# Half 1 of the tokens projected first, MLP halves renamed, and the operands of the MLP's first turn split between its stages

## The chip, the cores and the metric

The kernel runs on one core of one Trainium2 chip. The metric is the device time of one execution in microseconds (us). The engines are TensorE (PE: matrix products and transposes; PEld is its weight load), VectorE (DVE), ScalarE (ACT), GpSimd (POOL) and SyncE (SP), which here issues nearly all DMAs. Each engine works through its own instructions in order and waits for semaphores of the others.

## The reference

One layer of a streaming encoder trunk on 1024 tokens of width 1024, in float32, with RMS norms ahead of each part:

```python
for _ in range(DEPTH):
    h = h + parallel_mixer(rms_norm(h, norm_mix_g), w_in, ...)
    h = h + memory_cross_attention(rms_norm(h, norm_xattn_g), rms_norm(mem, norm_mem_g), ...)
    u = jax.nn.relu(rms_norm(h, norm_mlp_g) @ mlp_w1)
    h = h + (u * u) @ mlp_w2
```

The mixer holds eight heads of forgetting attention and four of gated linear attention. The cross-attention has four heads of 256 and ends in `o @ wo`, a product of 1024 x 1024 x 1024. The MLP has a hidden width of 4096: `mlp_w1` is 1024 x 4096, `mlp_w2` 4096 x 1024, with a squared ReLU between.

## The kernel before

**Products.** Every float32 operand is split into a high and a low part (`evac_split`, `split_into`): ScalarE copies it into the high part (L1038), VectorE subtracts that to get the low part (L1039). A product is then three matmuls of 128 x 128 by 128 x 512: high by high (L107), high weight by low operand (L108), low weight by high operand (L109). Tokens stand on the free axis in two halves of 512, and `h[:, k, half]` is the block of 128 rows k of the residual.

**Order.** A tile framework schedules the program from the order in which it is written and its own model of durations. It fixes the order of instructions on each engine and puts in the waits. Tiles come from pools; a new tile in a pool, or in a room that a closed pool has left, waits until the readers of the old one are done. SyncE's DMAs wait in one queue in their order.

**Cross-attention** (`xattn`). Eight units (n, u), two heads by four quarters of the tokens, are attended in turn. Each writes its output to DRAM (`od`, L1003), split into `o` high and low. `load_o` reads one half of the tokens back as `oh`, `ol`.

**The o-projection** (`project_o_first`, `project_o_rest`). 16 blocks of 24 matmuls: weights `Wo` (rows 0 to 3 of h) and `W` (rows 4 to 7), each by two halves of the tokens. Before, half 0 is finished first, by both, and then half 1 by `W` (rows 4 to 7) and by `Wo` (rows 0 to 3). `finish` adds the squares of a block into `acc` (ScalarE L165, GpSimd L166), writes the block to DRAM for the last addition (`hd`), and scales it for the MLP (L883). `token_squares` reduces `acc` to a norm per token with four transposes (L173).

**The MLP** (`mlp`). Each product is a Winograd form of Strassen's scheme with seven products in place of eight (`products7`): the operand's quarters give b11, b21, b22 and t1 to t4, the weight's give a11, a12, a22 and s1 to s4, and `STAGES` lists which pairs are multiplied, in which order, and into which kind of bank (x, w or y; banks of a kind go on accumulating). A stage has two weights i and, in the first layer, 12 matmuls for each. The first layer has eight turns p of seven stages, 168 matmuls each. The second has five chunks of 4, 3, 3, 3 and 3 hidden blocks, each with two turns, 168 or 126 matmuls. `hidden` and `output` take each bank away after its stage; the first layer's output goes to DRAM (`ud`) and comes back as operands of the second. `weights7` loads a turn's two weight tensors into `raw7` (1 MB or 768 KB each), splits the quarters, and makes s1 to s4 with sums (L1065, L1066, L1071, L1072, on VectorE in the first layer, on GpSimd in the second). Its generator yields twice, and `prep` runs it whole.

**Operands of the first turn.** b11 and b21 are split as soon as half 0 is projected. Then come, in each of the last four blocks, L841 (the block's sum), L883, L909, L910, L913, L914 and L912 on VectorE, which make four of the operands in the room of h and the low part of t2. `mlp` then splits t1, t3, b22 and t4 whole (128 x 2048 each) before the first turn.

Of the kernel before, what the change touches and what calls it, by code (L numbers as in the profile page):

```python
# [51 lines left out]
class Layer:  # L52
# [798 lines left out]
    def project_o_rest(self, mx):

# [3 lines left out]
        with ExitStack() as st:  # L856
# [28 lines left out]
            for k in range(KT):  # L885
                finish(k, 0, h(k, 0), k == 0)
                if k % 4 == 3:
                    self.operand(("b11", "b21")[k // 4], x0, self.h[:, k - 3:k + 1, 0:512])
            self.token_squares(0, self.yv[:, 0:4])
# [10 lines left out]
            next(self.W1)  # L900

            X = self.X["t2"] = self.T(x0, [P, 2, 4, 512], F32R, "x7")
            for i in range(4):
# [1 line left out]
                self.o_block(self.Wo, 0, 1, i, next(banks), t)
                finish(i, 1, t, False)
                t2 = self.T(self.s7, [P, 2, 512], F32, "s7")[:, 0, :]
                b11, b21, b12, b22 = h(i, 0), h(4 + i, 0), h(i, 1), h(4 + i, 1)
                nc.vector.tensor_tensor(b11, b12, b11, ALU.subtract)  # L909
                nc.vector.tensor_tensor(t2, b22, b11, ALU.subtract)  # L910
                nc.scalar.activation(X[:, 0, i], t2, AF.Copy)
                nc.vector.tensor_tensor(X[:, 1, i], t2, f(X[:, 0, i]), ALU.subtract)  # L912
                nc.vector.tensor_tensor(b12, b22, b12, ALU.subtract)  # L913
                nc.vector.tensor_tensor(b21, b21, t2, ALU.subtract)  # L914
            self.XB["t2"] = [X[:, 0, i] for i in range(4)], [X[:, 1, i] for i in range(4)]
# [7 lines left out]
    def xattn(self):  # L923
        nc = self.nc
        with ExitStack() as st:
# [80 lines left out]
            units = [(n, u) for n in range(2) for u in range(4)]  # L1006
            q = []
            for i, (n, u) in enumerate(units):
                if u == 0:
# [32 lines left out]
    def weights7(self, srcs, n, eng):  # L1042
# [14 lines left out]
        for src, o in zip(srcs, out):  # L1057
            raw = self.T(self.raw7, [P, 4, 512], F32, "raw7")[:, :, 0:n]
            nc.sync.dma_start(raw, src)
# [206 lines left out]
```

## Time and profile before

| | |
|---|---|
| median of 3 runs | 1486.61 us (1486.08 to 1487.83) |
| the profiled execution | 1480.27 us |
| its span in the trace | 1478.6 us |
| mean granted TensorE clock | 0.988 |
| end of the o-projection, start of the MLP's first turn | about 847 us |
| DMA, mean over the span | 151 GB/s, 223.94 MB |

The trace is of one execution, and its times count from the start of the span. An engine's row gives the time in which it was busy; the granted clock is the share of full speed at which TensorE was allowed to run. A wait is put down to the instruction that released it, with the line of the kernel. Stretches of the span have their own busy times; a timeline lists single instructions with the idle time ahead of them in brackets.

### The profile page before, as it was taken

To read this page: it belongs to the slowest core of one execution; us is meant where nothing else is said; L and a number is where in the kernel's file an instruction comes from. 1 tells how busy PE (TensorE), PEld (TensorE's weight loads), DVE (VectorE), ACT (ScalarE), POOL (GpSimd) and SP (SyncE) were. 2 spreads that over 40 slices of the span, in tenths; PEclk is the share of its full clock that TensorE was granted. 3 is DMA by queue.
4 is the path that set the end of the run, shared out by engine and by line. 5 is a ranking of instruction groups with operands and counts; after the bars stand their busy time and mean duration, and the time that the engine had idled before them with its cause. 6 is when DMAs were issued, how large, how long until landed. Compare 5 with 4: busy or idle time off the path is not lost.

```text
span 1478.6 us, 19173 instructions
## 1 busy us (share of the span) xinstructions
PE 1430.0 (97%) x7058; PEld 1195.3 (81%) x7058; DVE 920.8 (62%) x1322; ACT 681.2 (46%) x1092; POOL 430.8 (29%) x457
## 2 busy tenths in 40 slices
PE   7999999999998998999999979999999999999998
PEld 6777788887887787888888868888888888888886
DVE  4396422427776676656654875765565848788686
ACT  4473332326776555445442344544444736335230
POOL 3157503323463412522212300000000342433454
PEclk9999999999999999999999989999999999999999
DMA  8424530259677752413285113544444846337353
GB/s 273 122 54 121 143 86 1 72 173 261 187 203 193 192 158 74 155 40 104 72 279 219 52 63 146 210 171 171 170 169 149 291 159 229 129 109 233 113 201 114
DMA packets 125118, 223.94 MB, mean 151 GB/s; under 512 B 8384, under 2 KB 66528, under 8 KB 118368
## 3 DMA queue, kind: packets, MB, share of 16 engines
q1 hardware_dynamic: 125024, 222.71, 47.0%
q8 instruction: 56, 0.92, 0.2%
q14 instruction: 38, 0.31, 0.1%
HBM read 150.59 MB, written 72.09 MB: 151 GB/s over the span
## 4 chain that ended last, share of the span: by engine, by line
PE 78%; DMA 8%; DVE 7%; ACT 3%; issue 1%; POOL 1%; SPq 0%; POOLq 0%; ACTq 0%; DVEq 0%
PE mm L107 13%; PE mm L108 12%; PE mm L109 12%; PE my L109 7%; PE my L107 7%; PE my L108 7%; PE tr L107 3%; PE tr L108 3%; PE tr L109 3%; DMA raw<-in_w_in_dram 2%; DMA raw<-in_xattn_wkv_dram 2%; PE tr L661 1%; PE pv L668 1%; PE pv L669 1%; PE s L621 1%
## 5 line engine op out<-in xcount | busy, mean ns | idle before, releaser
L109 PE MATMUL my<-x,g 128*128 128x512 f32 x472 | 184.7, 392 | 5.9 <-DVE g L1039 5.8
L107 PE MATMUL my<-x,g 128*128 128x512 f32 x472 | 185.0, 392 | 2.8 <-ACT g L1038 2.8
L108 PE MATMUL my<-x,g 128*128 128x512 f32 x472 | 184.6, 391 | 0.0
L1065 POOL TENSOR_TENSOR s<-raw 128x384 f32<-128x384 f32 (+1 forms) x20 | 25.9, 1297 | 372.0 <-DMA raw<-in_mlp_w_dram 341.4
L1038 ACT ACTIVATE g<-s 128x1024 fp32r<-128x1024 f32 (+1 forms) x72 | 69.0, 963 | 132.8 <-PE my L109 62.3
L108 PE MATMUL mm<-wl,xh 128*128 128x512 f32 x320 | 126.5, 396 | 3.6 <-DVE wl L97 3.6
L107 PE MATMUL mm<-wh,xh 128*128 128x512 f32 x320 | 127.4, 400 | 1.4 <-DVE sq L298 1.4
L109 PE MATMUL mm<-wh,xl 128*128 128x512 f32 x320 | 126.3, 395 | 0.0
L109 PEld LDWEIGHTS my<-x,g 128*128 128x128 f32 x472 | 89.1, 189 | 25.5 <-DVE g L1039 7.0
L107 PEld LDWEIGHTS my<-x,g 128*128 128x128 f32 x472 | 89.2, 189 | 21.8 <-ACT g L1038 3.0
L108 PEld LDWEIGHTS my<-x,g 128*128 128x128 f32 x472 | 89.2, 189 | 18.5
L1039 DVE TENSOR_TENSOR g<-s,g 128x1024 fp32r<-128x1024 f32 (+1 forms) x72 | 85.0, 1186 | 11.1 <-ACT g L1038 10.7
L107 PE MATMUL mm<-x,g 128*128 128x512 f32 x228 | 89.3, 392 | 0.0
L108 PE MATMUL mm<-x,g 128*128 128x512 f32 x228 | 89.2, 391 | 0.0
L109 PE MATMUL mm<-x,g 128*128 128x512 f32 x228 | 88.8, 390 | 0.0
L632 POOL TENSOR_SCALAR p<-p,rrec 128x128 f32<-128x128 f32 (+3 forms) x64 | 50.8, 796 | 128.0 <-DVE rrec L631 115.4
L1039 DVE TENSOR_TENSOR g<-raw,g 128x1024 fp32r<-128x1024 f32 (+3 forms) x72 | 65.4, 910 | 34.2 <-ACT g L1038 34.2
L1178 DVE TENSOR_TENSOR x<-x 128x1024 fp32r<-128x1024 f32 (+1 forms) x64 | 74.4, 1184 | 11.4 <-ACT x L1177 11.1
L97 DVE SCALAR_TENSOR_TENSOR wl<-raw,cols,wh 128x512 fp32r<-128x512 f32 x64 | 49.8, 816 | 48.0 <-ACT wh L96 42.8
L1038 ACT ACTIVATE g<-raw 128x1024 fp32r<-128x1024 f32 (+3 forms) x72 | 55.2, 769 | 48.2 <-PE my L109 20.6
L107 PE MATMUL mm<-wh,sh 128*128 128x512 f32 x192 | 76.3, 399 | 0.7 <-DVE mkv L118 0.4
L108 PE MATMUL tr<-x,g 128*128 128x512 f32 x196 | 76.2, 389 | 0.0
(309 smaller groups left out, 3786.5 us busy)
## 6 DMA issues: line engine op xcount, KB each, us to landing
ud<-h SPq DMA_DIRECT2D x32, 1024.0 KB
x<-ud SPq DMA_DIRECT2D x48, 512.0 KB
raw<-in_mlp_w_dram SPq DMA_DIRECT2D x20, 1024.0 KB
raw<-in_mlp_w_dram SPq DMA_DIRECT2D x16, 768.0 KB
raw<-in_w_in_dram SPq DMA_DIRECT2D x23, 512.0 KB
raw<-in_xattn_wkv_dram SPq DMA_DIRECT2D x16, 512.0 KB
od<-o SPq DMA_DIRECT2D x32, 256.0 KB
xt<-in_x_dram SPq DMA_DIRECT2D x8, 512.0 KB
```

Of the source, the lines that this page charges most:

```text
L97: nc.vector.scalar_tensor_tensor(wl, r, g, f(wh), ALU.mult, ALU.subtract)
L107: mm(ps, lh[k], rh[k], start=start and k == 0, stop=False, **kw)
L108: mm(ps, lh[k], rl[k], start=False, stop=False, **kw)
L109: mm(ps, ll[k], rh[k], start=False, stop=stop and k == n - 1, **kw)
L621: nc.tensor.matmul(ps[:, c], qa[:, ts], ka[:, c], start=True, stop=False)
L632: nc.gpsimd.tensor_scalar(p[:, 0:n], p[:, 0:n], rr, 1.0, ALU.mult, ALU.mult)
L661: nc.tensor.transpose(o, pp[i][:, kb * P:(kb + 1) * P], self.ident)
L668: nc.tensor.matmul(pv, va[:, kb, :], th[:, js], start=kb == 0, stop=False)
L1038: self.nc.scalar.activation(hi, src, AF.Copy)
L1039: self.nc.vector.tensor_tensor(lo, src, f(hi), ALU.subtract)
L1065: eng.tensor_tensor(s[:, 0], raw[:, 3], raw[:, 2], ALU.add)
L1178: nc.vector.tensor_tensor(lo, f(lo), f(hi), ALU.subtract)
```

## The change

Six things change together; every matrix product stays.

1. *Half 1 first.* The units of the second pair of heads are attended in the order 2, 3, 0, 1, `load_o` takes half 1 first, and the o-projection finishes half 1 before half 0. The last four blocks are rows 0 to 3 of half 0.
2. *Halves renamed.* The two halves of the MLP's inner dimension change names: b11 is now made of rows 4 to 7 of half 0 (before: rows 0 to 3), and the first layer's weights are stored in another order (`swapped`).
3. *b11 and t2 early.* Both are made and split block by block in the four blocks of `W` with half 0. The last four blocks only have their sum and their scaling.
4. *STAGES in another order*: before b11, b21, t2, t1, t3, b22, t4; now b11, t1, t2, b22, t3, b21, t4. `weights7` splits a11 first, then s1 and s2, s3 and s4, and a12 and a22 last; before, a11 and a12 came first and a22 last.
5. *Operands between the stages.* A generator `first_turn` splits t1 before the first turn and t3, b22, b21 and t4 after the first stages of it; `token_squares` of the last half moves to turn 1 and the spread of the factors F to turn 3.
6. *Rooms.* x0 has 2 tiles and x1 5 (before 3 and 4), `g74` opens earlier, and in the second layer the rooms are grouped as (b11, t1), (b22, t2), (b21, t3), (t4). The map from products to output quarters follows the new names.

```diff
-            self.load_o(op1, 1)
+            self.load_o(op1, 0)
             for i in range(4):
-                self.o_block(W, 1, 0, i, next(banks))
+                self.o_block(W, 1, 1, i, next(banks))
...
             for i in range(4):
                 t = self.T(xp, [P, 512], F32, "h2", bufs=2)
-                self.o_block(W, 1, 1, i, next(banks), t)
-                finish(4 + i, 1, t, i == 0)
+                self.o_block(W, 1, 0, i, next(banks), t)
+                finish(4 + i, 0, t, i == 0)
+                t2 = self.T(xp, [P, 512], F32, "t2", bufs=2)
+                b11, b12, b22 = h(4 + i, 0), h(4 + i, 1), h(i, 1)
+                self.evac_split(X1[:, 0, i], X1[:, 1, i], b11)
+                nc.vector.tensor_tensor(b11, b12, b11, ALU.subtract)
+                nc.vector.tensor_tensor(t2, b22, b11, ALU.subtract)
+                self.evac_split(X2[:, 0, i], X2[:, 1, i], t2)
+                nc.vector.tensor_tensor(b12, b22, b12, ALU.subtract)
...
-    STAGES = (("x", "a11", "b11"), ("w", "a12", "b21"), ("x", "s2", "t2"), ("y", "s1", "t1"), ("x", "s3", "t3"),
-              ("y", "s4", "b22"), ("x", "a22", "t4"))
+    STAGES = (("x", "a11", "b11"), ("y", "s1", "t1"), ("x", "s2", "t2"), ("y", "s4", "b22"), ("x", "s3", "t3"),
+              ("w", "a12", "b21"), ("x", "a22", "t4"))
...
-            g(o, ("a11", "a12"), raw[:, 0:2])
+            g(o, ("a11",), raw[:, 0:1])
             raws.append(raw)
-        yield
...
-            g(o, ("a22",), raw[:, 2:3])
-        yield out
+        for raw, o in zip(raws, out):
+            g(o, ("a12", "a22"), raw[:, 1:3])
+        yield
...
+        def first_turn():
+            self.operand("t1", x1, half(4, 0))
+            yield
+            self.operand("t3", x1, half(4, 1))
+            next(self.W1)
+            yield
+            self.operand("b22", x1, half(0, 1))
+            yield
+            t4 = half(0, 0)
+            self.operand("b21", x1, t4)
+            for j in range(2):
+                nc.vector.tensor_tensor(t4, t4, f(X["t2"][:, j]), ALU.subtract)
+            yield
+            self.operand("t4", x1, t4)
...
+            def taken(i, j, ps):
+                hidden(i, j, ps)
+                if p == 0 and i == 1:
+                    next(turn, None)
+
+            self.products7(A, B, 4, taken)
+            if p == 1:
+
+                self.token_squares(0, self.yv[:, 0:4])
```

In the fences below, x7 are operands, g1 and g2 weights split (one quarter, or a pair), s7 the weights' sums, raw7 the weights as loaded, and my and mm the banks of TensorE. Lines of the changed program are one or two lower than before for the same operation.

**TensorE, behind the first stages of the first turn.** Before, after b21 and the four transposes (x7_1876 is t2, x7_1903 is t1, g2_1894 and g2_1896 are s1 and s2 of the two weights):

```order
L109 MATMUL my_1910_8621<-x7_1858_8206,g2_1875_8360 128x512
L173 MATMUL tr_1913_8783<-ident_14_73,acc_1849_8161 128x128 [waits PE_49,Pool_49]
L173 MATMUL tr_1913_8783<-ident_14_73,acc_1849_8161 128x128 x3
L107 MATMUL my_1907_8579<-x7_1876_8363,g2_1894_8540 128x512 [waits Activation_49]
L108 MATMUL my_1907_8579<-x7_1876_8363,g2_1894_8540 128x512
L107 MATMUL mm_1911_8661<-x7_1903_8567,g2_1894_8540 128x512
L108 MATMUL mm_1911_8661<-x7_1903_8567,g2_1894_8540 128x512 [waits DVE_49]
L107 MATMUL my_1908_8593<-x7_1876_8363,g2_1896_8546 128x512 [waits Activation_49]
L108 MATMUL my_1908_8593<-x7_1876_8363,g2_1896_8546 128x512
L107 MATMUL mm_1912_8675<-x7_1903_8567,g2_1896_8546 128x512
L108 MATMUL mm_1912_8675<-x7_1903_8567,g2_1896_8546 128x512
L109 MATMUL my_1907_8579<-x7_1876_8363,g2_1894_8540 128x512 [waits DVE_49]
```

The changed program, from the last matmul of b11 on (x7_1896 is t1, g2_1881 and g2_1883 are s1 and s2 of the two weights):

```order
L109 MATMUL my_1898_8565<-x7_1859_8211,g1_1879_8391 128x512
L107 MATMUL my_1906_8600<-x7_1896_8548,g2_1881_8397 128x512 [waits DVE_49,Activation_49]
L107 MATMUL my_1907_8614<-x7_1896_8548,g2_1883_8403 128x512 [waits DVE_49]
L108 MATMUL my_1906_8600<-x7_1896_8548,g2_1881_8397 128x512 [waits DVE_49]
L109 MATMUL my_1906_8600<-x7_1896_8548,g2_1881_8397 128x512
L107 MATMUL my_1906_8600<-x7_1896_8548,g2_1881_8397 128x512
```

The third stage's first matmuls, with t2, waited for s2 and its low half; now t1 follows b11 at once, in the second stage, and the third matmul of that stage waits for t1's low half. The transposes are gone from here.

**ScalarE and VectorE, around the last block of the projection.** ScalarE before (from the squares of the last block on; x7_1876 is t2, x7_1903 to x7_1906 are t1, t3, b22 and t4):

```order
L165 ACTIVATE sqT_1891_8508<-h2_1889_8481 128x512 [waits DVE_49,Pool_49]
L1038 ACTIVATE x7_1903_8567<-h_1369_5812 128x2048 [waits DVE_49]
L911 ACTIVATE x7_1876_8363<-s7_1892_8513 128x512 [waits DVE_49]
L1038 ACTIVATE x7_1904_8570<-h_1369_5812 128x2048 [waits DMAHW3_49,DMAHW4_49,DMAHW2_49,DMAHW5_49,DMAHW1_49,DMAHW6_49,DMAHW0_49,DMAHW7_49,DVE_49,Pool_49]
L1038 ACTIVATE x7_1905_8573<-h_1369_5812 128x2048
L1038 ACTIVATE x7_1906_8576<-h_1369_5812 128x2048 [waits DVE_49]
L1131 ACTIVATE h_1369_5812<-my_1907_8579 128x512 [waits DVE_49,PE_49]
L1131 ACTIVATE h_1369_5812<-my_1908_8593 128x512 [waits PE_49]
L1038 ACTIVATE g2_1894_8540<-s7_1893_8537 128x1024 [waits DVE_49]
L1038 ACTIVATE g2_1896_8546<-s7_1895_8543 128x1024 [waits DVE_49]
L1038 ACTIVATE g2_1899_8555<-s7_1897_8549 128x1024 [waits DVE_49,PE_49]
```

and now (g2_1902 and g2_1903 are s3 and s4, x7_1896, x7_1899, x7_1908 and x7_1909 are t1, t3, b22 and b21):

```order
L165 ACTIVATE sqT_1892_8497<-h2_1890_8470 128x512 [waits DVE_49,Pool_49]
L1037 ACTIVATE g2_1902_8588<-s7_1900_8582 128x1024 [waits DMAHW5_49,DMAHW7_49,DMAHW2_49,PE_49]
L1037 ACTIVATE g2_1903_8591<-s7_1901_8585 128x1024
L165 ACTIVATE sqT_1895_8529<-h2_1893_8502 128x512 [waits DVE_49,Pool_49]
L1037 ACTIVATE x7_1896_8548<-h_1369_5812 128x2048
L1037 ACTIVATE x7_1899_8579<-h_1369_5812 128x2048 [waits DMAHW4_49,DMAHW6_49,DMAHW1_49,PE_49]
L1037 ACTIVATE x7_1908_8628<-h_1369_5812 128x2048 [waits DMAHW3_49,DMAHW4_49,DMAHW2_49,DMAHW5_49,DMAHW1_49,DMAHW6_49,DMAHW0_49,DMAHW7_49,DVE_49,Pool_49]
L1037 ACTIVATE x7_1909_8657<-h_1369_5812 128x2048
L1149 ACTIVATE h_1369_5812<-my_1897_8551 128x512 [waits DVE_49,PE_49]
```

VectorE before, in the same place:

```order
L1066 TENSOR_TENSOR s7_1893_8537<-s7_1893_8537,raw7_1872_8353 128x512 [waits DVE_49]
L912 TENSOR_TENSOR x7_1876_8363<-s7_1892_8513,x7_1876_8363 128x512 [waits Activation_49]
L1066 TENSOR_TENSOR s7_1895_8543<-s7_1895_8543,raw7_1874_8358 128x512 [waits DVE_49]
L1039 TENSOR_TENSOR x7_1904_8570<-h_1369_5812,x7_1904_8570 128x2048 [waits DMAHW3_49,DMAHW2_49,Activation_49]
L1039 TENSOR_TENSOR x7_1905_8573<-h_1369_5812,x7_1905_8573 128x2048 [waits Activation_49]
L1071 TENSOR_TENSOR s7_1897_8549<-raw7_1872_8353 128x512 [waits DVE_49]
L1072 TENSOR_TENSOR s7_1897_8549<-raw7_1872_8353,s7_1893_8537 128x512
L1039 TENSOR_TENSOR x7_1906_8576<-h_1369_5812,x7_1906_8576 128x2048 [waits Activation_49]
L1139 TENSOR_TENSOR h_1369_5812<-my_1909_8607,h_1369_5812 128x512 [waits PE_49,Activation_49]
L175 TENSOR_REDUCE ss4_1914_8788<-tr_1913_8783 128x4 [waits PE_49]
L1139 TENSOR_TENSOR h_1369_5812<-my_1910_8621,h_1369_5812 128x512 [waits Activation_49]
L1039 TENSOR_TENSOR g2_1894_8540<-s7_1893_8537,g2_1894_8540 128x1024 [waits Activation_49]
```

and now, from the last block's sum on:

```order
L841 TENSOR_TENSOR h2_1893_8502<-mm_1894_8503,h_1369_5812 128x512 [waits DMAHW1_49,PE_49,Activation_49]
L883 SCALAR_TENSOR_TENSOR h_1369_5812<-h2_1893_8502,cols_13_72,sB_1811_7964 128x512 [waits DVE_49]
L1038 TENSOR_TENSOR g2_1902_8588<-s7_1900_8582,g2_1902_8588 128x1024 [waits Activation_49]
L1038 TENSOR_TENSOR g2_1903_8591<-s7_1901_8585,g2_1903_8591 128x1024 [waits Activation_49]
L1038 TENSOR_TENSOR x7_1896_8548<-h_1369_5812,x7_1896_8548 128x2048 [waits Activation_49]
L1038 TENSOR_TENSOR x7_1899_8579<-h_1369_5812,x7_1899_8579 128x2048 [waits Activation_49]
L1038 TENSOR_TENSOR x7_1908_8628<-h_1369_5812,x7_1908_8628 128x2048 [waits DMAHW3_49,DMAHW2_49,Activation_49]
L1038 TENSOR_TENSOR x7_1909_8657<-h_1369_5812,x7_1909_8657 128x2048 [waits Activation_49]
L1129 TENSOR_TENSOR h_1369_5812<-h_1369_5812,x7_1860_8212 128x4x512 [waits DVE_49]
```

Before, the four operands stood ahead of the low halves of s1 and s2 (g2_1894, g2_1896). Now s1 and s2 are split earlier, in the four blocks of W; behind the last block come s3 and s4, whose first high half waits for TensorE, then t1, and the other operands behind it.

**SyncE and ScalarE, in the cross-attention.** The first weights of the MLP, SyncE before:

```order
L1003 DMA od_8_64<-o_1600_6888 128x2x256 [waits DMAHW7_49,DVE_49]
L1003 DMA od_8_64<-o_1656_7104 128x2x256 [waits DMAHW0_49,Activation_49]
L1003 DMA od_8_64<-o_1656_7104 128x2x256 [waits DMAHW1_49,DVE_49]
L1003 DMA od_8_64<-o_1658_7122 128x2x256 [waits DMAHW2_49,Activation_49]
L1003 DMA od_8_64<-o_1658_7122 128x2x256 [waits DMAHW3_49,DVE_49]
L1003 DMA od_8_64<-o_1692_7295 128x2x256 [waits DMAHW4_49,Activation_49]
```

and now:

```order
L1002 DMA od_8_64<-o_1600_6888 128x2x256 [waits DMAHW7_49,DVE_49]
L1002 DMA od_8_64<-o_1656_7104 128x2x256 [waits DMAHW0_49,Activation_49]
L1058 DMA raw7_1876_8384<-in_mlp_w1_dram 128x2048 [waits DMAHW1_49,PE_49]
L1002 DMA od_8_64<-o_1656_7104 128x2x256 [waits DMAHW2_49,DVE_49]
L1002 DMA od_8_64<-o_1658_7122 128x2x256 [waits DMAHW3_49,Activation_49]
L1002 DMA od_8_64<-o_1658_7122 128x2x256 [waits DMAHW4_49,DVE_49]
L1058 DMA raw7_1878_8389<-in_mlp_w1_dram 128x2048 [waits DMAHW5_49]
```

and ScalarE now, with the split of the first of them:

```order
L114 ACTIVATE o_1658_7122<-pv_1657_7109 128x512 [waits DMAHW4_49,DMAHW6_49,PE_49,Activation_49]
L984 ACTIVATE p_1687_7267,rs2_1688_7268<-s_1685_7252,nm2_1686_7265 128x256 [waits DVE_49,Pool_49]
L984 ACTIVATE p_1687_7267,rs2_1688_7268<-s_1685_7252,nm2_1686_7265 128x256
L1037 ACTIVATE g1_1877_8386<-raw7_1876_8384 128x512 [waits DMAHW1_49]
L114 ACTIVATE qh_1659_7128<-tr_1676_7213 128x512 [waits PE_49]
L114 ACTIVATE th_1677_7220<-tr_1684_7245 128x512 [waits PE_49]
L783 ACTIVATE sh_1733_7510<-h_1369_5812 128x1024 [waits PE_49,Activation_49]
L140 ACTIVATE qn_1700_7349<-mm_1699_7324 128x512 [waits PE_49,Activation_49]
```

The two loads stood behind the first loads of the o-projection's second half; now they stand between the writes of o, and their splits between the cross-attention's own operations.

More of the change, by code (lines that the diff above doesn't have):

```diff
@@ L833, in load_o @@
             self.nc.sync.dma_start(f(ol[:, k, :]), self.od[:, 1, half, k, :])
-        self.O.append(([oh[:, k, :] for k in range(KT)], [ol[:, k, :] for k in range(KT)]))
+        self.O[half] = [oh[:, k, :] for k in range(KT)], [ol[:, k, :] for k in range(KT)]
     def o_block(self, W, n, half, i, ps, out=None):
@@ L885, in project_o_rest @@
             for k in range(KT):
[L886 to L889, printed above, removed]
+                finish(k, 1, h(k, 1), k == 0)
+            self.token_squares(1, self.yv[:, 4:8])
+            X1, X2 = (self.T(x0, [P, 2, 4, 512], F32R, "x7") for _ in range(2))
+            self.X = {"b11": X1, "t2": X2}
+            self.XB = {n: tuple([X[:, j, i] for i in range(4)] for j in range(2)) for n, X in self.X.items()}
             for i in range(4):
                 t = self.T(xp, [P, 512], F32, "h2", bufs=2)
-                self.o_block(W, 1, 1, i, next(banks), t)
-                finish(4 + i, 1, t, i == 0)
+                self.o_block(W, 1, 0, i, next(banks), t)
[7 more added lines that the diff above has]
+                nc.vector.tensor_tensor(b12, b22, b12, ALU.subtract)
             wst.close()
             self.raw7 = self.open(mx, "raw7", 2, side="right", **kw)
+            self.g4p = self.open(mx, "g74", 2, side="right", **kw)
             self.ga = self.open(mx, "g7a", 2, side="right", **kw)
@@ L899, in project_o_rest @@
             self.W1 = self.weights7([self.w1[q] for q in range(2)], 512, nc.vector)
-            next(self.W1)
-            X = self.X["t2"] = self.T(x0, [P, 2, 4, 512], F32R, "x7")
+            self.A = next(self.W1)
             for i in range(4):
                 t = self.T(xp, [P, 512], F32, "h2", bufs=2)
[L905 to L915, printed above, removed]
+                self.o_block(self.Wo, 0, 0, i, next(banks), t)
+                finish(i, 0, t, False)
     def operand(self, key, pool, src):
@@ L1004, in attend @@
                                                   u % 2 * 256:u % 2 * 256 + 256], f(o[:, i]))
[L1006 removed]
+            units = [(0, u) for u in range(4)] + [(1, u) for u in (2, 3, 0, 1)]
             q = []
             for i, (n, u) in enumerate(units):
[L1009 removed]
+                if i % 4 == 0:
                     weights(n)
@@ L1068, in weights7 @@
             sa.append(s)
+        yield out
         for raw, o, s2 in zip(raws, out, sa):
@@ L1111, in prep @@
             w = self.weights7(srcs, n, eng)
+            A = next(w)
             next(w)
-            return next(w)
-        A = next(self.W1)
-        for key, k, half in (("t1", 0, 0), ("t3", 0, 1), ("b22", 4, 1), ("t4", 4, 0)):
-            self.operand(key, x1, h[:, k:k + 4, half * 512:(half + 1) * 512])
+            return A
+        half = lambda k, i: h[:, k:k + 4, i * 512:(i + 1) * 512]
+        def first_turn():
[12 more added lines that the diff above has]
+            self.operand("t4", x1, t4)
+        turn = first_turn()
+        next(turn)
+        A = self.A
         h4 = h.rearrange("p k s -> p (k s)").rearrange("p (b c s) -> p b c s", b=4, s=512)
@@ L1197, in output @@
                 def output(i, j, ps):
-                    k, half = ((0, 0), (0, 0), (0, 1), (1, 1), (1, 1), (0, 1), (1, 0))[j]
+                    k, half = ((0, 0), (1, 1), (0, 1), (0, 1), (1, 1), (0, 0), (1, 0))[j]
                     k, ts = 2 * (o + i) + k, slice(half * 512, (half + 1) * 512)
                     y = h[:, k, ts]
-                    if first and j in (0, 2, 3, 6):
+                    if first and j in (0, 1, 2, 6):
                         nc.scalar.activation(y, ps, AF.Copy)
@@ L1204, in output @@
                         nc.vector.tensor_tensor(y, ps, y, ALU.add)
-                    if last and j in (1, 4, 5, 6):
+                    if last and j in (3, 4, 5, 6):
                         nc.vector.tensor_tensor(y, y, F[:, half], ALU.mult)
```

34 lines of the change are left out of this document (15 added, 19 removed).

## Prediction

> **What bounds the kernel now.** I read the page first, then busy time by stretches, then TensorE's waits, then the timelines of the one place that is left. The page's row of engines says what kind of kernel this is.
>
> ```profile
> PE 1430.0 (97%) x7058; PEld 1195.3 (81%) x7058; DVE 920.8 (62%) x1322; ACT 681.2 (46%) x1092; POOL 430.8 (29%) x457
> ```
>
> TensorE is busy 97% of the span. The change leaves every matrix product in place, so it can only win where TensorE stands or runs slowly. Busy time by stretches (columns: PE, PEld, DVE, ACT, POOL, granted clock, DMA share, GB/s) finds that place.
>
> ```profile
> 840.00:850.00 10.00, 10.00 (x46) 8.26 (x44) 9.86 (x15) 3.69 (x6) 1.31 (x2) 1.00 0.08 29
> 850.00:860.00 10.00, 8.76 (x41) 7.07 (x39) 9.97 (x13) 8.33 (x7) 2.79 (x1) 1.00 0.07 26
> 860.00:870.00 10.00, 3.27 (x8) 2.06 (x8) 10.00 (x9) 3.47 (x5) 0.19 (x1) 0.61 0.29 106
> 870.00:880.00 10.00, 9.45 (x31) 7.62 (x32) 6.39 (x11) 3.20 (x4) 0.00 (x0) 0.71 0.29 105
> 900.00:1180.00 280.00, 279.92 (x1241) 231.57 (x1240) 176.86 (x222) 145.25 (x177) 12.99 (x8) 1.00 0.51 190
> 1180.00:1470.00 290.00, 289.91 (x1280) 239.73 (x1279) 218.38 (x261) 108.65 (x137) 115.22 (x85) 1.00 0.49 164
> ```
>
> From 900 to 1470 us TensorE misses 0.17 us: nothing to win there, only to lose. Between 850 and 880 it runs 80 matmuls where full rate gives some 45 in 10 us, and VectorE is busy without a break from 840 to 870. TensorE's waits from 840 to 1475 us are two:
>
> ```profile
> PE my L109 <- DVE g L1039: 5.8, 1, 5.8
> PE my L107 <- ACT g L1038: 2.8, 1, 2.8
> ```
>
> TensorE's timeline (start, us, operation, idle before) shows them, and what follows each.
>
> ```profile
> 857.25 0.39 PE L109 MATMUL my<-x,g 128*128 128x512 f32 x1
> ...
> 857.93 0.39 PE L109 MATMUL my<-x,g 128*128 128x512 f32 x1
> 858.16 0.60 PE L173 MATMUL tr<-ident,acc 128*128 128x128 f32 x4
> 861.51 0.50 PE L107 MATMUL my<-x,g 128*128 128x512 f32 x1 [2.76 <-ACT g L1038]
> ...
> 864.15 0.63 PE L108 MATMUL mm<-x,g 128*128 128x512 f32 x1
> 870.55 0.80 PE L109 MATMUL my<-x,g 128*128 128x512 f32 x1 [5.78 <-DVE g L1039]
> 871.15 0.63 PE L107 MATMUL my<-x,g 128*128 128x512 f32 x1
> ...
> 874.99 0.63 PE L109 MATMUL mm<-x,g 128*128 128x512 f32 x1
> 875.41 0.57 PE L107 MATMUL mm<-x,g 128*128 128x512 f32 x1
> 875.82 0.39 PE L108 MATMUL mm<-x,g 128*128 128x512 f32 x1
> ```
>
> At full clock matmuls start (857.93 - 857.25) / 3 = 0.227 us apart; after the two gaps they start 0.42 to 0.43 us apart (874.99 to 875.41), with the granted clock at 0.61 and 0.71. The place is the MLP's first turn, two stages in: 48 matmuls (from 858.16 - 48 x 0.227 = 847.3 on) are done, those of b11 and b21, and stage 2 waits for the split of s2, then of its low half. **The loss:** from 858.16 to 875.82 are 17.66 us. In them are four transposes (0.60) and 20 matmuls, which need 20 x 0.227 = 4.54. So 17.66 - 0.60 - 4.54 = 12.5 us are lost, about 8.5 in gaps and 4 to slow clock.
>
> **The change, part by part.** VectorE is what is late. Its timeline there:
>
> ```profile
> 832.67 1.81 DVE L909 TENSOR_TENSOR h<-h 128x512 f32<-128x512 f32 x1
> 848.48 0.69 DVE L841 TENSOR_TENSOR h<-mm,h 128x512 f32<-128x512 f32 x1
> 849.68 0.75 DVE L883 SCALAR_TENSOR_TENSOR h<-h,cols,sB 128x512 f32<-128x512 f32 x1
> 850.94 0.69 DVE L909 TENSOR_TENSOR h<-h 128x512 f32<-128x512 f32 x1
> 855.68 2.28 DVE L1039 TENSOR_TENSOR x<-h,x 128x2048 fp32r<-128x2048 f32 x1
> 859.68 4.48 DVE L1039 TENSOR_TENSOR x<-h,x 128x2048 fp32r<-128x2048 f32 x2
> 865.29 2.28 DVE L1039 TENSOR_TENSOR x<-h,x 128x2048 fp32r<-128x2048 f32 x1
> 869.29 3.48 DVE L1039 TENSOR_TENSOR g<-s,g 128x1024 fp32r<-128x1024 f32 x3
> ```
>
> Before, four operands (t1, t3, b22, t4: 2.28 + 4.48 + 2.28 = 9.0 us) stand ahead of the low half of s2, at 869.29, which stage 2 needs at 858. Every block of the projection also brings seven VectorE operations (L841, L883, L909, L910, L913, L914, L912), so VectorE enters the turn late: the last block's L841 starts at 848.48, though its matmuls had ended by 847.3.
>
> *Half order, t2 and b11 early.* In the changed program the last four blocks have two VectorE operations each, 0.69 + 0.75 = 1.44 us of the 24 x 0.227 = 5.45 us that a block takes on TensorE. The subtractions and the splits of b11 and t2 stand in the four blocks ahead, some 0.69 + 0.75 + 5 x 0.69 = 4.9 us a block, 6.0 with one slow operation like that at 832.67: up to 2 us behind after four blocks, made up in the first of the last four. So b11 and s1 are there when the last block ends, and stage 0 begins as before at 847.3. I cost this at nothing; the cover is the 4 us a block that VectorE has over.
>
> *Stage 1 now needs t1*, and t1 is late, as the rows of the order show: on ScalarE two splits of s3 and s4 stand ahead, and the first of them waits for the last block's matmul (its room lies on that of the attention output). ScalarE's durations, and two of GpSimd's additions, whose like falls in the middle of it:
>
> ```profile
> L1038 ACT ACTIVATE x<-h x6: 1892/1914/1924, 808.6 to 857.7; 128x2048 fp32r<-128x2048 f32 x6
> L1038 ACT ACTIVATE g<-s x72: 829/1044/1067, 860.4 to 1452.3; 128x1024 fp32r<-128x1024 f32 x40, 128x768 fp32r<-128x768 f32 x32
> 849.26 0.63 ACT L165 ACTIVATE sqT<-h 128x512 f32<-128x512 f32 x1 [0.63 <-DVE h L841]
> 832.65 1.29 POOL L166 TENSOR_TENSOR acc<-acc,sqT 128x512 f32<-128x512 f32 x1 [1.98 <-ACT sqT L165]
> 849.97 2.82 POOL L166 TENSOR_TENSOR acc<-acc,sqT 128x512 f32<-128x512 f32 x1 [4.49 <-ACT sqT L165]
> ```
>
> From 847.3: 2 x 1.04, then 0.63, then t1's high half 1.91, ends at 851.9; VectorE meanwhile does 0.69 + 0.75 + 2 x 1.16 (3.48 / 3), till 851.1, and then t1's low half, 2.28, till 854.2. The first matmul that needs that low half follows 24 + 2 matmuls after 847.3, at 853.2. The stall is 1.0 us undisturbed. GpSimd's addition falls among these VectorE operations, and L909 took 1.81 at 832.67 beside such an addition and 0.69 at 850.94, 1.1 more: at most 2.1. **I take 1.3 us**, nearer to the undisturbed end, because part of the addition can fall in the time in which VectorE waits for ScalarE anyway. The trace's shortest gap that a slow pitch follows is 2.76 us, so for 1.3 I count no slow clock.
>
> The Trainium skill, "SBUF — State Buffer", section "SBUF: two separate sides", says that a VectorE operation with two SBUF inputs and a GpSimd operation that reads SBUF shut each other out for a whole instruction. By that rule t1's low half could wait for a whole addition (1.29 us at 832.65), and the sum would be a gain of 10 us and not 11; the 1.81 against 0.69 agrees with it.
>
> *The other operands come between the stages.* Stages last 24 x 0.227 = 5.45 us, so after the stall stages 2 to 6 begin at about 859.5, 864.9, 870.4, 875.8 and 881.3. Stage 2 (s2, t2) has all. VectorE goes on with t3 (to 856.5), b22 (858.8, needed 864.9) and b21 (861.1, needed 875.8); between them ScalarE's x at 1.91 each keep ahead. Then come two subtractions of 128x2048 (nearest row 2.28 each) and two splits of weights, to some 868; t4's split stands on VectorE behind an operation on the next turn's first weights, needed at 881.3. The price of a load:
>
> ```profile
> 920.88 1.66 SPq L1059 DMA_DIRECT2D raw<-in_mlp_w_dram  x2
> 925.90 1.06 ACT L1038 ACTIVATE g<-raw 128x1024 fp32r<-128x1024 f32 x1 [1.96 <-DMA raw<-in_mlp_w_dram]
> 930.05 1.06 ACT L1038 ACTIVATE g<-raw 128x1024 fp32r<-128x1024 f32 x1 [3.09 <-DMA raw<-in_mlp_w_dram]
> ```
>
> One weight tensor lands 5.0 us after issue, the second behind it 9.2. The next turn's first load goes out once both of this tensor's last splits are done, about 866, lands at 871, and t4 is ready at 874: 7 us to spare. These cost nothing.
>
> *token_squares to turn 1, spread to turn 3.* Four transposes move with their 0.60 us: no change in the sum. Each adds a bank to the cycle, bounded by the 0.08 us that TensorE misses from 900 to 1180 now and one VectorE operation of 0.7 that a matmul would wait for: -0.1 to +0.7 each. I take 0, since all that these rows show missing is nearer to it.
>
> *The first two weight loads move from about 777 to about 708 us*, into the cross-attention; past them on SyncE's queue go seven writes of o and the loads of the o-projection. Rows there:
>
> ```profile
> 707.35 2.46 SPq L1003 DMA_DIRECT2D od<-o  x4
> 713.89 0.60 ACT L114 ACTIVATE qh<-tr 128x512 fp32r<-128x512 f32 x1 [2.76 <-PE tr L963]
> 720.97 0.27 PE L107 MATMUL s<-kT,qh 128*128 128x256 f32 x1
> ```
>
> On ScalarE the split of the first load stands right ahead of the qh at 713.89, on VectorE its low half ahead of ql. Issued at 707.7, it lands at 712.7 alone, and at 715 if the writes share; qh then moves from 713.9 to 715.6 and is wanted by TensorE at 720.97. Nothing to 2 us; I take 0. The first load of the o-projection's second half of operands now waits for every write of o. No row shows that wait; a 512 KB load would take half of the 5.0 us above, so I bound it by 0 and 2.5, and take 0, since the projection's first half covers it.
>
> **Sum:** 12.5 - 1.3 = 11.2 us gained. The profiled execution took 1480.27 (span 1478.6 and 1.7 around it), so 1469.1 there; against the median of 1486.61 it is **1475.4**.
>
> **Rivals.**
>
> *The clock falls again.* ScalarE's two splits ahead of t1, GpSimd's addition and waits between engines add up to a gap of 2.8 us or more instead of 1.3. After such a gap the trace has 12 matmuls at 0.43 (870.55 to 875.41: 4.9 us where 2.7 do), and 8 with 2.6 where 1.8 do. So 3 for the gap and 3 for the clock: gain 6.5, **1480**. For it: the order rows; against: 1.0 by rows alone. The Trainium skill, "TensorE: Matmul & The Clock Gate", section "Part 1: The HAM clock gate", gives a free-running window of about 3.4 us after which the clock halves; by that rule a gap near 1.3 keeps full clock, yet the trace's slow pitch follows 2.76 us of idleness after 0.60 of transposes, so I don't rely on the exact length.
>
> *The early loads or the o loads are late.* ScalarE held to 718 and beyond, or the o operands by 2 to 3 us: gain 8.5, **1478**. Against it: 715.6 leaves 5 us to 720.97.
>
> *The splits pile up further on.* The change removes no split; if t3, b22 or t4 come late for their stage, 3 to 4 us return: **1479**. Against it: 4 us of slack at the tightest.
>
> *Slower: the weights of every turn come late.* A raw tile is now given back only when the last pair (a12, a22) has been split, which waits for room until stage 2 of its turn is over. A turn of 3 blocks has 126 matmuls, 28.6 us, a stage 4.1. Release at 12.3 + 1.3, the second load 9.2 on, at 22.8; the sums on GpSimd and splits, priced by
>
> ```profile
> 1211.71 1.01 POOL L1065 TENSOR_TENSOR s<-raw 128x384 f32<-128x384 f32 x1 [11.19 <-DMA raw<-in_mlp_w_dram]
> 1212.80 1.35 POOL L1066 TENSOR_TENSOR s<-s,raw 128x384 f32<-128x384 f32 x1
> ```
>
> and some 2 more, end at 27.5; needed at stage 1 of the next turn, 28.6 + 4.1 = 32.7. Slack 5 us, less where loads of x stand ahead in SyncE's queue. From 5 us later on each turn stalls, and above 11.2 / 17 = 0.66 us for each of 17 turns the change loses; 1.0 each gives **1492**. Against it: a DMA share of about 0.5 in both long stretches.
>
> **How the numbers follow.** Forecast 0.60; clock 0.12; loads 0.06; pile-up 0.06; two of these together, about 1485, 0.08; late weights 0.08. A measurement of this kernel tells 0.2%, 3 us, from no change. Faster 0.60 + 0.12 + 0.06 + 0.06 = 0.84, same 0.08, slower 0.08. The range starts where the whole 12.5 and up to 1 us of other small losses come back, 1473, and ends beyond the clock's rival at 1482, which leaves out 0.16 above.
>
> **What would show it.** Right: TensorE's only wait of the first turn is for VectorE's t1 low half near 853, 1 to 2 us, pitch 0.227 throughout, granted clock 1.00 in 860 to 880, and the turn ends 11 us earlier. Wrong: a granted clock below 1 at 855 to 865 (clock), a TensorE wait at 714 to 730 or near 787 (loads), waits on x or h splits at 865 to 885 (pile-up), or waits of TensorE for g behind raw in every later turn (late weights).

## The result, and the profile of the changed kernel

The changed kernel takes 1495.35 us (median of 4 runs, 1494.12 to 1498.03), the kernel of before beside it 1486.34: 9.0 us slower, ratio 1.0066 (1.0044 to 1.0088). The forecast was 1475.4. The profiled execution took 1494.93 us, its span is 1493.2, the granted clock 0.99.

TensorE's row of the page, and its busy time by stretches (columns as before: PE, PEld, DVE, ACT, POOL, clock, DMA share, GB/s):

```profile
PE 1434.6 (96%) x7058; PEld 1195.3 (80%) x7058; DVE 931.7 (62%) x1323; ACT 681.6 (46%) x1095; POOL 432.4 (29%) x457
```

```profile
850.00:860.00 10.00, 8.69 (x39) 6.89 (x38) 7.71 (x6) 8.03 (x7) 2.12 (x2) 1.00 0.08 29
860.00:870.00 10.00, 10.00 (x46) 8.28 (x45) 9.71 (x6) 5.31 (x7) 0.00 (x0) 1.00 0.00 0
870.00:880.00 10.00, 10.00 (x46) 8.29 (x45) 9.02 (x10) 5.80 (x6) 0.00 (x0) 1.00 0.60 210
880.00:1140.00 260.00, 260.00 (x1158) 215.53 (x1157) 152.22 (x201) 127.78 (x153) 0.56 (x1) 1.00 0.44 168
1140.00:1180.00 40.00, 35.92 (x152) 29.25 (x152) 37.73 (x35) 27.41 (x33) 14.89 (x8) 0.96 0.81 298
1240.00:1484.00 244.00, 232.99 (x1008) 189.14 (x1007) 190.85 (x229) 80.52 (x103) 95.88 (x72) 0.99 0.43 147
```

The hole at 860 to 880 is gone: 92 matmuls in 20 us at full clock. New holes are 4.1 us at 1140 to 1180, where the first layer ends and the second begins, and 11.0 us between 1240 and 1484, in stretches that missed nothing before. TensorE's waits, first from 845 to 1240 us, then from 1240 on:

```profile
PE mm L109 <- DVE g L1038: 4.1, 1, 4.1
PE my L108 <- DVE x L1038: 1.3, 1, 1.3
...
PE mm L107 <- DVE h L1228: 5.7, 3, 3.7
PE tr L107 <- DVE h L1228: 3.7, 2, 2.7
PE my L107 <- DVE h L1228: 1.5, 3, 1.1
```

L1228 is VectorE's addition of a finished bank to h: TensorE stands because a bank hasn't been taken away. The waits of these three rows lie in the first turns of the second layer's later chunks, where operands are reloaded, or in the last chunk.

Profiled executions reach the MLP at different times (845.3 to 855.1 us in the kernels below), though the instructions up to about 700 us are the same in all. So I compare the MLP alone: from the start of its first matmul to the start of its last, with what TensorE lost there against full pitch (0.227 us a matmul, summed over all starts; gaps under 0.12 left out; the sums are good to about 0.3 us). Before it is 624.9 us, now 634.8: 9.9 us more, where 9.0 were measured.

| kernel | median, us (before beside it) | ratio (95%) | MLP | lost: first turn | change of layers | behind |
|---|---|---|---|---|---|---|
| before | 1486.34 | 1 | 624.9 | 12.6 | 0.2 | 0.0 |
| changed | 1495.35 (1486.34) | 1.0066 (1.0044 to 1.0088) | 634.8 | 1.5 | 5.8 | 14.0 |
| after_again | 1494.59 (1485.66) | 1.0068 (1.0045 to 1.0091) | 634.0 | 1.5 | 6.1 | 13.6 |
| new_front_old_weights | 1480.01 (1485.40) | 0.9957 (0.9940 to 0.9973) | 623.1 | 5.2 | 5.8 | 0.0 |
| new_front_role_rooms | 1481.11 (1485.40) | 0.9972 (0.9955 to 0.9989) | 618.6 | 1.0 | 4.6 | 0.3 |
| old_front_new_weights | 1514.70 (1485.40) | 1.0181 (1.0155 to 1.0207) | 652.7 | 15.3 | 6.0 | 15.0 |
| before_late_release | 1486.88 (1485.40) | 1.0004 (0.9988 to 1.0020) | 625.0 | 9.8 | 2.4 | 0.7 |
| after_no_sums | 1483.73 (1485.66) | 0.9988 (0.9966 to 1.0010) | 623.4 | 1.5 | 5.8 | 3.9 |
| after_no_reload | 1481.58 (1485.66) | 0.9981 (0.9966 to 0.9995) | 620.5 | 1.7 | 5.8 | 1.3 |
| after_sums_on_vector | 1493.69 (1485.66) | 1.0046 (1.0019 to 1.0072) | 632.9 | 1.5 | 1.4 | 17.1 |
| role_rooms_o_swapped | 1480.46 (1485.65) | 0.9972 (0.9956 to 0.9989) | 618.2 | 1.0 | 4.0 | 0.7 |
| old_weights_o_swapped | 1478.72 (1485.65) | 0.9950 (0.9933 to 0.9968) | 617.9 | 5.4 | 0.4 | 0.0 |

**One stall followed back.** The largest, 3.65 us, is in the first turn of the third chunk. SyncE's queue in the turn ahead of it, then GpSimd, ScalarE, VectorE and TensorE of the changed kernel (start, us, operation):

```profile
1287.75 0.55 SPq L1058 DMA_DIRECT2D raw<-in_mlp_w_dram  x1
1288.39 1.24 SPq L1200 DMA_DIRECT2D x<-ud  x2
1290.71 0.55 SPq L1058 DMA_DIRECT2D raw<-in_mlp_w_dram  x1
```

```profile
1300.07 1.03 POOL L1063 TENSOR_TENSOR s<-raw 128x384 f32<-128x384 f32 x1 [4.88 <-DMA raw<-in_mlp_w_dram]
1301.06 1.02 POOL L1070 TENSOR_TENSOR s<-raw 128x384 f32<-128x384 f32 x1
1302.04 1.33 POOL L1071 TENSOR_TENSOR s<-raw,s 128x384 f32<-128x384 f32 x1
1303.33 2.00 POOL L1064 TENSOR_TENSOR s<-s,raw 128x384 f32<-128x384 f32 x1
```

```profile
1305.37 1.58 ACT L1037 ACTIVATE g<-s 128x768 fp32r<-128x768 f32 x2 [1.57 <-POOL s L1064]
```

```profile
1289.70 0.95 DVE L1038 TENSOR_TENSOR g<-raw,g 128x768 fp32r<-128x768 f32 x1
...
1303.02 1.44 DVE L1202 TENSOR_TENSOR x<-x 128x1024 fp32r<-128x1024 f32 x1
1304.37 0.68 DVE L1228 TENSOR_TENSOR h<-mm,h 128x512 f32<-128x512 f32 x1
1304.97 1.44 DVE L1202 TENSOR_TENSOR x<-x 128x1024 fp32r<-128x1024 f32 x1
1306.34 3.44 DVE L1038 TENSOR_TENSOR g<-s,g 128x768 fp32r<-128x768 f32 x2
1309.70 1.21 DVE L1202 TENSOR_TENSOR x<-x 128x1024 fp32r<-128x1024 f32 x1
1310.84 0.68 DVE L1228 TENSOR_TENSOR h<-mm,h 128x512 f32<-128x512 f32 x1
```

```profile
1311.66 0.47 PE L107 MATMUL mm<-x,g 128*128 128x512 f32 x1 [3.65 <-DVE h L1228]
```

The second raw load goes out at 1290.71, right behind VectorE's half of the last split of the tile it replaces (1289.70). It lands at 1300.0. GpSimd then makes s1 and s2 of that tensor in two steps, but the two sums of the other tensor's s3 and s4 (L1070, L1071) stand between, so they end at 1305.3. VectorE splits s1 and s2 until 1308.1 (the first of the two in its row), then s3 and s4 of the other tensor until 1309.8, then one operand, and only then adds the bank that TensorE waits for. The addition itself needs nothing of these weights: the last matmul into that bank, the end of the turn before, started at 1302.9, but VectorE, busy without a break, came to the addition at 1310.84. The weights alone would have been just in time: the stalled matmuls are those of the second weight's s1, and the first to read its low half was due at 1308.3.

### The profile page after: what moved, and what is told of

Read it like the earlier page. It is cut to its first block, busy times and chain, and to the rows that moved or that the text cites. A ratio compares the mean times of both kernels' runs of the same rounds, so it can differ in the third digit from the quotient of the medians.

```text
span 1493.2 us, 19162 instructions
## 1 busy us (share of the span) xinstructions
PE 1434.6 (96%) x7058; PEld 1195.3 (80%) x7058; DVE 931.7 (62%) x1323; ACT 681.6 (46%) x1095; POOL 432.4 (29%) x457
## 4 chain that ended last, share of the span: by engine, by line
PE 72%; DMA 10%; DVE 9%; POOL 3%; ACT 3%; issue 3%; SPq 0%; POOLq 0%; DVEq 0%; ACTq 0%
PE mm L107 13%; PE mm L108 12%; PE mm L109 12%; PE my L108 5%; PE my L107 5%; PE my L109 5%; PE tr L107 3%; PE tr L108 3%; PE tr L109 3%; DMA raw<-in_mlp_w_dram 2%; DMA raw<-in_w_in_dram 2%; DMA x<-ud 2%; PE tr L661 1%; DVE g L1038 1%; DVE x L1202 1%
## 5 line engine op out<-in xcount | busy, mean ns | idle before, releaser
L1063 POOL TENSOR_TENSOR s<-raw 128x384 f32<-128x384 f32 (+1 forms) x20 | 22.7, 1136 | 409.7 <-DMA raw<-in_mlp_w_dram 376.4
L1038 DVE TENSOR_TENSOR g<-raw,g 128x1024 fp32r<-128x1024 f32 (+3 forms) x72 | 72.1, 1003 | 104.3 <-ACT g L1037 104.2
L1038 DVE TENSOR_TENSOR g<-s,g 128x1024 fp32r<-128x1024 f32 (+1 forms) x72 | 92.3, 1287 | 23.9 <-ACT g L1037 23.9
L107 PE MATMUL mm<-x,g 128*128 128x512 f32 x220 | 86.7, 394 | 5.7 <-DVE h L1228 5.7
L109 PE MATMUL mm<-x,g 128*128 128x512 f32 x220 | 86.5, 393 | 4.1 <-DVE g L1038 4.1
L108 PE MATMUL mm<-x,g 128*128 128x512 f32 x220 | 86.2, 392 | 0.0
L107 PE MATMUL tr<-x,g 128*128 128x512 f32 x204 | 80.4, 394 | 3.8 <-DVE h L1228 3.7
L1201 ACT ACTIVATE x<-x 128x1024 fp32r<-128x1024 f32 (+1 forms) x64 | 58.7, 946 | 49.6 <-DMA x<-ud 49.6
L109 PE MATMUL tr<-x,g 128*128 128x512 f32 x204 | 80.0, 392 | 0.0
```

The lines of the kernel that those rows point to most:

```text
L107: mm(ps, lh[k], rh[k], start=start and k == 0, stop=False, **kw)
L108: mm(ps, lh[k], rl[k], start=False, stop=False, **kw)
L109: mm(ps, ll[k], rh[k], start=False, stop=stop and k == n - 1, **kw)
L1038: self.nc.vector.tensor_tensor(lo, src, f(hi), ALU.subtract)
L1063: eng.tensor_tensor(s[:, 0], raw[:, 3], raw[:, 2], ALU.add)
L1201: nc.scalar.activation(hi, f(lo), AF.Copy)
```

## The experiments

**Front and weights apart.** new_front_old_weights keeps the half order, the early b11 and t2 and the split of the first turn's operands, and takes stages, pairs and rooms of before:

```diff
-    STAGES = (("x", "a11", "b11"), ("y", "s1", "t1"), ("x", "s2", "t2"), ("y", "s4", "b22"), ("x", "s3", "t3"),
-              ("w", "a12", "b21"), ("x", "a22", "t4"))
+    STAGES = (("x", "a11", "b11"), ("w", "a12", "b21"), ("x", "s2", "t2"), ("y", "s1", "t1"), ("x", "s3", "t3"),
+              ("y", "s4", "b22"), ("x", "a22", "t4"))
-            g(o, ("a11",), raw[:, 0:1])
+            g(o, ("a11", "a12"), raw[:, 0:2])
...
             g(o, ("s3", "s4"), s)
-        for raw, o in zip(raws, out):
-            g(o, ("a12", "a22"), raw[:, 1:3])
+            g(o, ("a22",), raw[:, 2:3])
```

> The changed kernel with the stages, the pairs of weights, the rooms of operands and the output map of before (b11, b21, t2, t1, t3, b22, t4); half order, early b11 and t2, and the split of the first turn's operands stay, with b21 now the operand of the second stage. Theory 'late weights' (raw rooms are given back only after the pair a12, a22 is split, at the end of stage 2 of their own turn, so the second layer's weights come late where operands are reloaded): TensorE's stalls behind 1140 us, 21 us in the changed kernel, go away, the first turn loses 1 to 3 us, time 1473 to 1478. Theory 'rest of the change' (half order, renaming, moved token_squares and spread, 5 rooms in x1): the stalls stay, 1490 to 1496.

Measured 1480.01: 5.4 us faster than before, where the changed kernel was 9.0 slower. Behind the change of layers nothing is lost. The loss belongs to the weights' part of the change, not to the front. The time is above the 1473 to 1478 expected, since b21's low half came 3.1 us late in the first turn (and half clock behind it), and one wait at the change of layers stayed. The opposite mixture, old_front_new_weights, is the kernel of before with the changed stages, pairs, rooms and output map:

> The kernel of before with only the stages, pairs of weights, operand rooms and output map of the changed one; half 0 first, operands all split ahead of the first turn. 'Late weights' (or 'stage order'): the first turn loses 12 us or more as before, the second layer some 20 us, 1500 to 1512. 'Rest of the change': 1484 to 1490, with no stalls behind 1140 us.

Measured 1514.70, 29 us slower and above the 1500 to 1512 expected: 15.0 us are lost behind 1240, as in the changed kernel, and the first turn is worse than before's (15.3, and waits of 2.7 us soon after): there 10.7 us are two waits at the second stage, for s1 and then for its low half, which stand behind the operands' splits.

**Release and need apart.** before_late_release holds the raw rooms of before as long as the change does and leaves the stages as they were:

```diff
-            g(o, ("a22",), raw[:, 2:3])
+            g(o, ("a12b", "a22"), raw[:, 1:3])
```

> The kernel of before with a22 split together with a12 once more into a room of pairs, which is free only after stage 3 of the turn; 0.4 us more for ScalarE and VectorE for each weight, nothing else moved. 'Late weights': raw rooms go back some 15 us later than before and the second layer stalls in each of its ten turns, 10 to 40 us in all, 1496 to 1526. 'Stage order' or 'rest of the change': within 3 us of before, 1484 to 1490.

Measured 1486.88, ratio 1.0004: no change. The theory that the late release alone costs 10 us or more fell. The loads are as late as in the changed kernel. At the same reload the second goes out 20.5 us into its turn, which begins at 1271.3 (17.8 in the changed kernel, 1.4 before):

```profile
1282.68 0.55 SPq L1059 DMA_DIRECT2D raw<-in_mlp_w_dram  x1
...
1291.73 0.55 SPq L1059 DMA_DIRECT2D raw<-in_mlp_w_dram  x1
```

GpSimd's sums there, and TensorE's only wait from 1240 us on:

```profile
1298.35 1.02 POOL L1065 TENSOR_TENSOR s<-raw 128x384 f32<-128x384 f32 x1 [5.80 <-DVE h L1204]
1299.33 1.74 POOL L1071 TENSOR_TENSOR s<-raw 128x384 f32<-128x384 f32 x1
1301.03 2.00 POOL L1072 TENSOR_TENSOR s<-raw,s 128x384 f32<-128x384 f32 x1
1302.98 1.73 POOL L1066 TENSOR_TENSOR s<-s,raw 128x384 f32<-128x384 f32 x1
```

```profile
PE tr L109 <- DVE g L1039: 0.5, 1, 0.5
```

But here a turn opens with two stages on loaded quarters, a11 and a12, which need no sum; s2 and s1 are due at the third and fourth stage, 8 and 12 us into a turn of 28.6, where the change wants s1 at the second, 4 us into it. The late release isn't quite free in the profile: 2.4 us are lost at the change of layers and 0.7 behind, against 2.8 less than before in the first turn. The other way round, new_front_role_rooms gives the rooms back early and keeps s1 and s2 at the second and third stage:

```diff
-    STAGES = (("x", "a11", "b11"), ("y", "s1", "t1"), ("x", "s2", "t2"), ("y", "s4", "b22"), ("x", "s3", "t3"),
-              ("w", "a12", "b21"), ("x", "a22", "t4"))
+    STAGES = (("x", "a11", "b11"), ("y", "s1", "t1"), ("x", "s2", "t2"), ("w", "a12", "b21"), ("y", "s4", "b22"),
+              ("x", "s3", "t3"), ("x", "a22", "t4"))
-                p = self.gps[self.ng % len(self.gps)]
-                self.ng += 1
+                p = self.gb if names[0] == "a12" else self.ga
...
+        for raw, o in zip(raws, out):
+            g(o, ("a12", "a22"), raw[:, 1:3])
         for raw, o, s2 in zip(raws, out, sa):
```

> The changed kernel with its pairs of weights, but rooms by role (a12 and a22 always in g7b, s1 to s4 in g7a), a12 and a22 split ahead of s3 and s4, and the stages b11, t1, t2, b21, b22, t3, t4, so that the room of a12 and a22 is free at the end of the turn before and the raw rooms go back some 12 us earlier. 'Late weights': the stalls of the second layer go, 1473 to 1478. 'Stage order' (it is the order b11, t1, t2 and the grouping of operand rooms that bring operands late): stalls of 10 us and more stay, 1485 to 1496.

Measured 1481.11, ratio 0.9972; TensorE waits for nothing behind 1240 us, and 0.3 us are lost. At the reload above the second load goes out 5.9 us into its turn. The time is above the 1473 to 1478 expected for late weights, as 4.6 us stay at the change of layers, and below the 1485 of the other theory. This kernel also moves the stages behind the third and regroups the operand rooms; what that does wasn't measured apart. So behind 1240 us, with an early need and an early release nothing is lost to speak of, with a late release and a late need 0.7 us, and with the change's early need and late release 14.

**What fills the time between release and need.** after_no_sums leaves GpSimd's sums out of the second layer and splits loaded quarters in their place:

```diff
+            if eng is nc.gpsimd:
+                s = raw[:, 0:2]
+            else:
```

> The changed kernel without GpSimd's sums in the second layer: s1 and s2 are split from the first two loaded quarters, s3 and s4 from the last two, so the sums are left out. Raw rooms go back as late as before, at the end of stage 2. In the changed kernel the second tensor's s1 and s2 are ready some 2.5 us after they are needed at a reload, of which GpSimd's sums take 5.3 us from landing to the last one needed. 'Late weights, a chain of load, sums and splits': without the sums the stalls behind 1240 us fall from 14 us to 0 to 3. 'Reloaded operands alone' (VectorE is full of operand splits and evacuations whatever the weights do): 10 us or more stay.

3.9 us stay of 14.0, a little above the 0 to 3 expected: the sums, with what they hold up, are some 10 of it, and the rest wasn't taken apart. (The 2.5 us after need in the expectation don't hold for the stall above, as its rows show: what came late there was the bank.) Its waits from 1240 us on:

```profile
PE mm L107 <- DVE h L1234: 2.0, 1, 2.0
PE tr L107 <- DVE h L1234: 1.5, 2, 0.9
```

after_no_reload takes the reloads away:

```diff
+            if q0:
+                B = {n: tuple([v[q % 4] for q in range(q0, q0 + nk)] for v in B0[n]) for n in B0}
+            else:
+                B = B0 = {}
-            for names, room, which in groups:
+            for names, room, which in groups if q0 == 0 else ():
```

> The changed kernel without the second layer's reloads behind the first chunk: the later chunks multiply the operands of the first, so 32 of the 48 operand loads and their splits are left out. Weights come as late as in the changed kernel. 'Late weights alone' (every turn late by its own chain): stalls stay at 5 us or more. 'Collision' (late weights stall only where ScalarE, VectorE and the queue also carry a chunk's reload): the 14 us behind 1240 go to 0 to 1.

1.3 us stay, all in the last chunk. The weights are still late, though not by as much: in the same turn the two loads go out 12.3 and 14.4 us in (14.8 and 17.8 in the changed kernel), and from the second chunk on no load goes out earlier than 12.3.

```profile
1284.07 2.58 SPq L1058 DMA_DIRECT2D raw<-in_mlp_w_dram  x2
```

So the late release costs only where a chunk's reload comes with it. The reload's operand loads, splits and evacuations delay the weights further and crowd ScalarE and VectorE; which of the two counts for more isn't told apart. after_sums_on_vector moves the sums:

```diff
-                                  nk * P, nc.gpsimd)
+                                  nk * P, nc.vector)
```

> The changed kernel with the second layer's sums on VectorE: eight operations of about 0.55 us more a turn there, none on GpSimd, and so no operation of one held up by the other. If the two engines' hold-ups (sums of 2.0 instead of 1.0 us, splits of 1.7 instead of 0.95) make most of the lateness: stalls fall to a third, 1478 to 1485. If the late release does: they stay within a third of the 14 us, 1490 to 1500.

1493.69, and 17.1 us lost behind: no better. So nothing here speaks for most of the lateness being that VectorE and GpSimd hold each other up; but VectorE also had the sums' work to do, so the two aren't told apart fully. The changed kernel beside these:

> The changed kernel once more, on the same chip as the three above: 1492 to 1498, stalls of about 21 us behind 1140 us, whatever the theory.

It came out as the first time, 1494.59, with 19.7 us lost behind 1140.

**The change of layers.** new_front_old_weights still lost 5.8 us there, in one wait of 2.7 us and the half clock behind it. ScalarE's copy that it waited for, and TensorE's wait:

```profile
1181.58 0.60 ACT L1227 ACTIVATE h<-my 128x512 f32<-128x512 f32 x1 [2.89 <-DMA ud<-h]
```

```profile
PE my L107 <- ACT h L1227: 2.7, 1, 2.7
```

The renaming has put the first layer's last differences into rows 0 to 3 of h, which are written to DRAM last, and the second layer's first copies go into these rows. Two kernels take rows 4 to 7 first:

```diff
-            for o in (0, 2):
+            for o in (2, 0):
```

> The new front with the weights of before, and the second layer's output rows 4 to 7 ahead of rows 0 to 3. There the one wait of TensorE at the change of layers (2.66 us, and some 3 more at half clock) was for ScalarE's copy, which waited for the write of h. If the renamed halves make that wait, it goes and the 5.8 us with it: 1473 to 1477. If not, 1478 to 1482.

> The kernel with rooms by role, and in the second layer the output rows 4 to 7 ahead of rows 0 to 3. With the renamed halves the first layer's last outputs stand in rows 4 to 7 (written to DRAM first) and their differences in rows 0 to 3 (written last), and the second layer's first copies into h wait for that write. If so, the waits of TensorE for ScalarE's copy behind the write of h at about 1187 us go, the 4.6 us lost between 1140 and 1190 fall to 3 to 4, time 1477 to 1481. If the loss there is VectorE's alone, nothing changes: 1479 to 1482.

With the weights of before the wait shrinks to

```profile
PE my L107 <- ACT h L1227: 0.3, 1, 0.3
```

and the loss there from 5.8 to 0.4 us. So its cause is which rows are filled first, and that the renaming has turned round: the kernel of before, with its own names and rows 0 to 3 first, lost 0.2. The MLP takes 617.9 us, 7.0 less than before; measured 1478.72, 6.9 less, ratio 0.9950: **the best of the kernels, ahead of both**. It is still above the 1473 to 1477 expected; the first turn's 5.4 us stayed. With rooms by role the swap made no difference (1480.46, a loss of 4.0 for 4.6): there the copy still waits 2.0 us for the write of h, ahead of which a load of weights has gone out on the same queue, and two splits of weights are waited for besides.

## Why the prediction was wrong

*The first turn: right.* The forecast stall was 1.3 us behind two matmuls of the second stage, for t1's low half. The changed kernel's TensorE and VectorE:

```profile
857.44 0.61 PE L107 MATMUL my<-x,g 128*128 128x512 f32 x2
859.36 0.50 PE L108 MATMUL my<-x,g 128*128 128x512 f32 x1 [1.31 <-DVE x L1038]
```

```profile
853.65 3.45 DVE L1038 TENSOR_TENSOR g<-s,g 128x1024 fp32r<-128x1024 f32 x2
857.03 8.88 DVE L1038 TENSOR_TENSOR x<-h,x 128x2048 fp32r<-128x2048 f32 x4
```

It is 1.31, the two splits of s3 and s4 took 3.45 where 2.3 was the undisturbed sum (GpSimd's addition, the 1.1 us of the bound), and the clock stayed. Of 12.6 us, 11.1 came back, against 11.2 forecast. The other operands were in time, and the pile-up didn't come. The first weight loads went out at 712 and 715 us and cost TensorE nothing visible around 710 to 740.

*The steps at nothing.* token_squares and spread cost nothing that shows: TensorE is busy 260.00 of 260 us from 880 to 1140. The o-projection waits 0.9 us for its operands, before 0.7. The renaming I passed over entirely: which rows of h the second layer fills first, and when their write ends, was not worked out. It made the wait of 2.7 us at the change of layers with the weights of before. In the changed kernel itself the wait there is another, 4.1 us for VectorE's split of weights, so late weights again. The renaming's wait lies right behind it: without GpSimd's sums (after_no_sums) TensorE waits there 4.1 us for ScalarE's copy behind the write of h, and the same 5.8 us are lost.

*The step that failed: the slack of the late weights.* The mechanism stands in the prediction as the slower rival, with its place and a chance of 0.08; its sum left 5 us of slack. The turn ahead of the stall above begins at 1272.96. There the second load went out 17.8 us into the turn and not 13.6, as operand splits and an evacuation stood ahead of the last split on VectorE. Its 9.2 us were right (landed at 27.0). From there to the end of the split of s1 and s2 it took 8.1 us where I had 4.7, for the sums of the other tensor in between and for operations that took longer (2.00 for the second sum, 1.8 for the split). They were ready at 35.2, not at 27.5 (the terms of the sum add to 27.2), and by the sum they were needed at 32.7: the slack was gone. I priced each operation alone, in a turn without a reload, and the ten turns alike; what counts is the queue of the reload turn. In a turn without a reload the sum holds: in after_no_reload the second load of this turn goes out at 14.4, and the split ends at 28.3.

I also took as needed only what the matmuls read. By that alone there would have been hardly a stall even here: the late tensor is the second weight's, whose low half is first read at 35.3. TensorE stopped for a bank, whose addition stood on VectorE behind splits and operands for 7 us and more. At the change of layers, where the bank was free, the late split itself cost the 4.1 us.

*The price of the rival* was wrong too: not 1 us in each of 17 turns, but 14 us in the four reloads and the last chunk. The argument against it, a DMA share of about 0.5, said nothing: the loads were late in starting, not in bandwidth.

## What to carry to other kernels

When a reordering moves a consumer earlier (here sums, from the third stage to the second) and the release of its source's buffer later, add up the whole way from release to need in the busiest turn, with what stands ahead on each engine's queue, and not in a mean turn. Either half alone cost next to nothing here; both together took back more than the whole gain. An in-order engine that both prepares operands and empties accumulators can turn a late operand into a stall of matmuls that don't need it, and a change of names decides which rows are still being written when the next stage fills them.
